# Norms without activation tables, normalisations fed between the gate's steps, and a stricter load order, in a one-layer decoder step

## The chip, the cores and the metric

One Trainium2 chip, all 8 cores, two dies (cores 0 to 3 and 4 to 7). Every core runs the same program on its own prompt of 2048 positions and 16 of the 128 sample rows; no data passes between cores. The time of a run is that of its slowest core, in microseconds of the device. Some runs fall into a second, slower state, in which the cores of a die have a lower granted clock: whole runs at 1229 to 1423 us. Engines are called PE (matrix), DVE (VectorE), ACT (ScalarE) and POOL (GpSimd). SBUF is a core's on-chip memory, PSUM the memory into which PE writes its sums.

## The reference, cut to what matters

```python
def rmsnorm(x, g):
    return x * rsqrt(mean(x * x, -1) + 1e-6) * g

xn = rmsnorm(h, g_mix); z = xn @ w_in                   # x_a B_a C_a | u v | g_a g_b
y_a = (b_a * dwconv3(c_a * x_a)) @ w_out_a
u, v = gelu(uv); v = rmsnorm(v, g_v)
y_b = (u * chunk_spatial(v)) @ w_out_b
h = h + (sigmoid(ga) * y_a + sigmoid(gb) * y_b) @ w_o
up = dwconv3(rmsnorm(h, g_ffn) @ w_up)
h = h + (gelu(fa) * fb) @ w_down
h = h + sigmoid(rmsnorm(h, g_ple) @ w_ple_gate) * (p @ w_ple)
y = rmsnorm(h, g_final)
```

So there are four norms over the 1024 channels on the residual stream: before the input projection (gain index 0), before the up-projection (1), before the gate (2) and at the end (3).

## The kernel before

A core makes two passes of 1024 positions (the first with the 16 sample rows), each cut into blocks of 384, 384 and 256 (or 272) columns. Channels lie on partitions, so `h` is 8 tiles of 128 channels. Weights stream as slabs through a ring of eight slots; a slab is loaded as soon as its slot is free and what `LOAD_AFTER` lists for it has landed. The program gives each engine its instructions as a queue; in the traces below an engine that waits for one holds all behind it.

A pass has these stages, by which the text below counts: the v projection with its spatial preparation (in pass 0 together with the start); then the convolution, the spatial gating, the merge and the output projection (called "conv to merge"); the up-projection; the down-projection; the gate. After the last gate stage only DVE and the stores are left: the tail.

The norm squares on ACT, adds the squares on POOL (or DVE), sums over partitions with matmuls with a matrix of ones, and takes the inverse root on ACT as exp(-0.5 ln x):

```python
def rstd(self, b):
    ...
    r, rr = rsR.get()
    P.op("act", ... r = Ln(pt + eps));  P.op("act", ... r = Exp(-0.5 * r))
    return r, rr

def to_xn(self, b, gi):                       # to_y does the same into h, and stores it
    r, rr = self.rstd(b)
    for k in range(8):
        P.op("dve", ... xn[k] = h[k] * g[gi, k] * r)
```

Ln and Exp are in another activation table than the tanh of the gate or the gelu of v, so each norm costs ACT a load of tables, and the next tanh or gelu another.

The start, and the loop of the gate:

```python
LOAD_AFTER[1] = [("h", 7, 0)]                 # slab 1 waits for all of the first block of x
load_h(0, block 0, 4); load_h(0, block 1, 4)
R.prefetch()                                  # slabs 0 .. 7
load_h(0, block 2, 2, <after slab 3>)
...
fn = Norm(p, "pool", delay=1)
for b in blocks:
    for i in range(8):
        # PE: gate projection and p @ w_ple; ACT: tanh; DVE: (tanh + 1) * pE
        P.op("dve", ... h[i] = 0.5 * tg + h[i])
        fn.add(i, b)                          # square and sum for the last norm
        if bi == 0 and i == 1: nrm.to_xn(b2, 2)
        if bi > 0 and i == 4:
            fn.to_y(blocks[bi - 1], 3, 2)
            if p == 0: load_h(1, blocks_of(1)[bi - 1], 2)
```

Of the kernel before, what the change touches and what calls it, by code (L numbers as in the profile page):

```python
# [162 lines left out]
def build_program():  # L163
# [9 lines left out]
    xt_d = [din("xt0", [128, 8, TT]), din("xt1", [128, 8, 1024])]  # L173
# [10 lines left out]
    yt_d = [dout("yt0", [128, 8, TT]), dout("yt1", [128, 8, 1024])]  # L184
# [5 lines left out]
    with es:  # L190
# [3 lines left out]
        h = sb("h", [128, 8, TT], F32)  # L194
# [14 lines left out]
        saT = sb("saT", [128, 8, 2, NS], F32)  # L209
        sfT = sb("sfT", [128, 44, 2, NS], F32)  # L210
        oAs = sb("oAs", [128, 8, NS], F32)
        oFs = sb("oFs", [128, 44, NS], F32)
# [22 lines left out]
        class PsRot:  # L235
            def __init__(self):
                self.i = 0

            def get(self):
                b = self.i % 8  # L240
                self.i += 1
                return ps[b], ("ps", b)
# [24 lines left out]
        def tiles_of(p):  # L267
            tl = [dict(t=t, rows=128, c0=t * 128, blk=t // 3) for t in range(8)]
            if p == 0:
                tl.append(dict(t=8, rows=NS, c0=1024, blk=2))  # L270
            return tl

# [90 lines left out]
        def proj(pt, ptr, wv, wres, u, p, b, halo=False):  # L363
            lo, hi = xcols(p, b, halo)
            bi = b["idx"]
            pairs = []
# [7 lines left out]
        class Norm:  # L374
            def __init__(self, p, eng, src=None, delay=0, early=False):
                self.early = early
                self.p, self.eng, self.delay, self.pe = p, eng, delay, False
                self.src = src or (lambda k, b: (h[:, k, b["c0"]:b["c0"] + b["n"] + b["s"]], [("h", k, b["idx"])]))
                self.cnt, self.slot, self.pend = {}, {}, []

            def add(self, k, b):
                self.pend.append((k, b))
# [3 lines left out]
            def _emit(self, k, b):  # L386
# [9 lines left out]
                if self.pe:  # L396
                    if q == 0:
                        self.bank = psR.get()
                    t, w = narR.get()
                    out = t.bitcast(BF16)[:, 0:N]  # L400
                    pt, ptr = self.bank
                    if q % 2:
                        P.op("dve", lambda e: e.tensor_tensor(out=out, in0=src, in1=src, op=ALU.mult), reads=rd, writes=w)
                    else:
                        P.op("act", lambda e: e.activation(out=out, in_=src, func=AF.Square), reads=rd, writes=w)
                    P.op("pe", lambda e: e.matmul(pt[:, 0:N], lhsT=ones[:], rhs=out, start=(q == 0), stop=(q == 7)),
                         reads=["ones"] + w, writes=[ptr])
# [9 lines left out]
                if 0 < q < 7:  # L417
# [9 lines left out]
            def rstd(self, b):  # L427
# [4 lines left out]
                pt, ptr = self.bank if self.pe else psR.get()  # L432
                if not self.pe:
                    group(pt[:, 0:N], [(ones[:], ssb[:, s, 0:N], [("ssb", s)]), (ones[:], sqb[:, s, 0:N], [("sqb", s)])], ["ones"], ptr)
                r, rr = rsR.get()
                P.op("act", lambda e: e.activation(out=r[:, 0:N], in_=pt[:, 0:N], func=AF.Ln, bias=epsT[:, 0:1]), reads=[ptr, "epsT"], writes=[rr])  # L436
# [3 lines left out]
            def to_xn(self, b, gi):  # L440
                bi, N = b["idx"], b["n"] + b["s"]
                r, rr = self.rstd(b)
                for k in range(8):
                    src, rd = self.src(k, b)
                    dst = xns[self.p][:, k, b["c0"] + 2:b["c0"] + 2 + N]
                    P.op("dve", lambda e, src=src, dst=dst, k=k: e.scalar_tensor_tensor(  # L446
                        out=dst, in0=src, scalar=gcol(gi, k), in1=r[:, 0:N], op0=ALU.mult, op1=ALU.mult),
                        reads=rd + [rr, "cst"], writes=[("xn", self.p, k, bi)])

            def to_y(self, b, gi, parts):  # L450
                bi, N, c0 = b["idx"], b["n"] + b["s"], b["c0"]
                r, rr = self.rstd(b)
                per = 8 // parts
                for q in range(parts):
                    for k in range(q * per, (q + 1) * per):
                        hv = h[:, k, c0:c0 + N]
                        P.op("dve", lambda e, hv=hv, k=k: e.scalar_tensor_tensor(  # L457
                            out=hv, in0=hv, scalar=gcol(gi, k), in1=r[:, 0:N], op0=ALU.mult, op1=ALU.mult),
                            reads=[("h", k, bi), rr, "cst"], writes=[("h", k, bi)])
                    store(yt_d[self.p][:, q * per:(q + 1) * per, c0:c0 + N], h[:, q * per:(q + 1) * per, c0:c0 + N],  # L460
                          f"y{bi}{q}", [("h", k, bi) for k in range(q * per, (q + 1) * per)])

        def load_h(p, b, parts, after=()):
            bi, N, c0 = b["idx"], b["n"] + b["s"], b["c0"]
            per = 8 // parts
            for q in range(parts):
                load(h[:, q * per:(q + 1) * per, c0:c0 + N], xt_d[p][:, q * per:(q + 1) * per, c0:c0 + N], f"h{bi}{q}",
                     [("h", k, bi) for k in range(q * per, (q + 1) * per)], reads=after)
# [9 lines left out]
        use_table(AF.Ln)  # L478
        LOAD_AFTER[1] = [("h", 7, 0)]
        load(cst[:], const_d[:, :], "cst", ["cst"])  # L480
        load_h(0, blocks_of(0)[0], 4)
        load_h(0, blocks_of(0)[1], 4)
        R.prefetch()
        load_h(0, blocks_of(0)[2], 2, R.item_slot[3][2])
# [13 lines left out]
        def setup_small():  # L498
# [3 lines left out]
            for j in range(8):  # L502
                P.op("pool", lambda e, j=j: e.tensor_scalar(out=Ds[:, j, :], in0=cst[0:NS, 204:220], scalar1=cst[0:NS, 196 + j:197 + j],
                                                            scalar2=None, op0=ALU.mult), reads=["cst"], writes=["Ds"])

# [132 lines left out]
        nextn = [None]  # L638
        for p in range(2):
# [3 lines left out]
            vit = None  # L643
# [7 lines left out]
            if p == 0:  # L651
                nrm = Norm(0, "dve")
# [8 lines left out]
                vit = [next_item() for _ in range(4)]  # L661
# [9 lines left out]
                v_of(2, 1)  # L671
                setup_small()
                setup_state()
                load(pT[:, :, :], pt_d[0][:, :, :], "pT", [("pT", b) for b in range(3)], eng="pool")
                P.op("pool", lambda e: e.tensor_copy(out=xns[1][:, :, 0:2], in_=xns[0][:, :, 1024:1026]),
                     reads=[("xn", 0, k, 2) for k in range(8)], writes=[("xnh", 1)])
            else:
                vit = [next_item() for _ in range(4)]
                for hf in range(2):
                    for bl in range(3):  # L680
                        v_of(bl, hf)
                        if hf == 0 and bl == 1:
# [338 lines left out]
```

## Time and profile before

| | before |
|---|---|
| time, median of 17 runs, slow ones included | 1226.59 us (1224.25 to 1310.7) |
| cores of the profiled run | 1215.5 to 1224.0 us |
| PE, DVE, ACT, POOL busy | 94, 57, 41, 30% |
| loads of activation tables on one core | 33 |

The profile's page gives busy shares and forty slices in time; the windows give busy time in chosen stretches; an engine's timeline lists its instructions in order, with the rest before each in brackets and what ended it; the waits sum those rests.

### The profile page before, as it was taken

The numbers are of one execution on the slowest core, as the hardware profiler recorded it, in microseconds if no ns is written. First come the engines' busy times: TensorE is split into PE (matmuls) and PEld (weight loads), VectorE is DVE, ScalarE is ACT, GpSimd is POOL, SyncE is SP. The second block draws the span as 40 slices with busy tenths as digits, with TensorE's granted clock in tenths as the row PEclk, the third lists the DMA queues.
The fourth block names the chain that finished last, engine by engine and source line by source line (L and its number), as shares of the span: only waits on it lengthen the run. The fifth ranks groups of instructions, "written<-read, shape, count | busy, mean of one in ns | idle before, by whom it ended". The sixth has DMA issues, their size and how long they took to land.

```text
span 1224.0 us, 24337 instructions; the slowest of 8 cores (1215.5 to 1224.0 us)
## 1 busy us (share of the span) xinstructions
PE 1146.2 (94%) x7852; PEld 761.5 (62%) x7852; DVE 701.0 (57%) x1354; ACT 497.3 (41%) x1031; POOL 362.8 (30%) x411
## 2 busy tenths in 40 slices
PE   4699999999999999999889999999998999999983
PEld 2566666666656666666467666666665666666642
DVE  3336674222589899534862567522248899951386
ACT  3552232121445565333566123211134555541264
POOL 3020101222534343355340010122243443334232
PEclk9899999999999999999889999999999999999997
DMA  9638562444464442665469736233335343135303
GB/s 190 156 51 107 84 104 41 69 70 70 70 98 71 77 70 48 138 117 108 69 165 195 160 70 120 54 70 70 70 70 87 70 87 71 25 74 97 70 16 138
DMA packets 46619, 109.68 MB, mean 90 GB/s; under 512 B 10240, under 2 KB 26112, under 8 KB 46496
## 3 DMA queue, kind: packets, MB, share of 16 engines
q0 software_dynamic: 22016, 82.86, 40.6%
q1 hardware_dynamic: 24480, 25.27, 7.7%
q8 instruction: 67, 1.10, 0.3%
q14 instruction: 56, 0.46, 0.1%
HBM read 181.01 MB, written 9.95 MB: 156 GB/s over the span
## 4 chain that ended last, share of the span: by engine, by line
PE 77%; DVE 8%; DMA 5%; ACT 4%; issue 4%; POOL 2%; DVEq 0%; SPq 0%; POOLq 0%; ACTq 0%
PE pq L356 66%; PE pq L837 10%; DVE s_xn L446 3%; DMA s_h<-xt 2%; DMA s_ring<-win 2%; DVE s_h L457 1%; POOL s_ss L419 1%; DVE s_wide L920 1%; ACT L436 1%; DVE s_h L922 1%; DMA s_wide<-gv 1%; ACT s_rsb L436 1%; PE pq L604 1%; ACT s_sq L416 1%; ACT s_rsb L437 0%
## 5 line engine op out<-in xcount | busy, mean ns | idle before, releaser
L356 PE MATMUL pq<-s_xn,s_ring 128*128 128x386 bf16 (+5 forms) x5184 | 791.4, 310 | 15.8 <-DVE s_wide L920 6.0
L356 PEld LDWEIGHTS pq<-s_xn,s_ring 128*128 128x128 bf16 x5184 | 500.8, 97 | 276.4 <-issue 25.4
L776 DVE SCALAR_TENSOR_TENSOR s_wide<-pq,s_cst,s_wide 128x384 f32<-128x384 f32 (+1 forms) x528 | 278.5, 568 | 30.6 <-ACT s_wide L768 2.2
L768 ACT ACTIVATE s_wide<-pq,s_cst 128x384 f32<-128x384 f32 (+1 forms) x264 | 137.3, 548 | 131.8 <-DVE s_wide L776 115.3
L783 POOL TENSOR_TENSOR s_R<-s_wide 128x1024 bf16<-128x1024 f32 x44 | 103.8, 2359 | 173.1 <-DVE s_wide L776 155.0
L837 PE MATMUL pq<-s_R,s_ring 128*128 128x384 bf16 (+2 forms) x1056 | 155.0, 309 | 0.0
L419 POOL TENSOR_TENSOR s_ss<-s_ss,s_sq 128x384 f32<-128x384 f32 (+2 forms) x105 | 99.0, 947 | 166.2 <-ACT s_sq L416 158.6
L633 DVE SCALAR_TENSOR_TENSOR s_wide<-s_wide,pq 128x384 f32<-128x384 f32 (+2 forms) x96 | 49.2, 513 | 172.8 <-PE pq L356 172.8
L837 PEld LDWEIGHTS pq<-s_R,s_ring 128*128 128x128 bf16 x1056 | 103.2, 98 | 50.8
L356 PE MATMUL pq<-s_R,s_ring 128*128 128x384 bf16 (+2 forms) x768 | 119.8, 309 | 0.0
L416 ACT ACTIVATE s_sq<-s_h 128x384 f32<-128x384 f32 (+2 forms) x120 | 57.5, 486 | 146.1 <-DVE s_h L843 70.3
L631 ACT ACTIVATE s_wide<-pq 128x384 f32<-128x384 f32 (+2 forms) x96 | 43.9, 458 | 176.8 <-PE pq L356 142.5
L356 PEld LDWEIGHTS pq<-s_R,s_ring 128*128 128x128 bf16 x768 | 75.0, 98 | 37.0
L635 POOL TENSOR_TENSOR s_xn<-s_wide 128x384 bf16<-128x384 f32 (+2 forms) x48 | 43.7, 911 | 166.6 <-DVE s_wide L633 166.6
L356 PE MATMUL pq<-s_ring,s_xn 128*128 128x256 bf16 (+1 forms) x544 | 74.7, 297 | 16.2 <-DVE s_xn L446 12.5
L446 DVE SCALAR_TENSOR_TENSOR s_xn<-s_h,s_cst,s_rsb 128x384 bf16<-128x384 f32 (+2 forms) x120 | 62.4, 592 | 40.7 <-ACT s_rsb L437 40.7
L843 DVE TENSOR_TENSOR s_h<-pq,s_h 128x384 f32<-128x384 f32 (+2 forms) x48 | 23.6, 513 | 99.1 <-PE pq L837 99.1
L356 PEld LDWEIGHTS pq<-s_ring,s_xn 128*128 128x128 bf16 (+1 forms) x544 | 56.4, 105 | 34.4 <-issue 24.1
L579 ACT ACTIVATE s_wide<-s_wide,s_cst 128x384 f32<-128x384 f32 (+1 forms) x48 | 27.8, 579 | 122.3 <-DVE s_wide L577 122.3
L581 DVE SCALAR_TENSOR_TENSOR s_wide<-s_wide,s_cst 128x384 f32<-128x384 f32 (+1 forms) x48 | 27.5, 573 | 38.0 <-ACT s_wide L579 36.8
L321 POOL DMA_DIRECT2D s_ring<-win x56 | 30.0, 543 | 63.2 <-PE pq L356 21.4
L782 ACT ACTIVATE s_wide<-s_wide 128x1024 f32<-128x1024 f32 x44 | 46.1, 1048 | 0.9 <-DVE s_wide L776 0.9
(97 smaller groups left out, 668.0 us busy)
## 6 DMA issues: line engine op xcount, KB each, us to landing
s_ring<-win POOLq DMA_DIRECT2D x56, 512.0 KB, 10.6
s_ring<-wup POOLq DMA_DIRECT2D x44, 512.0 KB, 9.0
s_ring<-wdn POOLq DMA_DIRECT2D x16, 704.0 KB, 8.3
yt<-s_h SPq DMA_DIRECT2D x8, 768.0 KB, 4.0
s_ring<-woa POOLq DMA_DIRECT2D x8, 512.0 KB, 11.3
s_ring<-wob POOLq DMA_DIRECT2D x8, 512.0 KB, 12.6
s_ring<-wo POOLq DMA_DIRECT2D x8, 512.0 KB, 11.0
s_ring<-wg POOLq DMA_DIRECT2D x8, 512.0 KB, 7.2
```

Source lines behind the costliest of these rows:

```text
L356: P.op("pe", lambda e, l=l, r=r, q=q: e.matmul(out, lhsT=l, rhs=r, start=(q == 0), stop=(q == n - 1)), reads=list(reads) + list(rd), write ...
L416: P.op("act", lambda e: e.activation(out=out, in_=src, func=AF.Square), reads=rd, writes=[w])
L419: P.op(self.eng, lambda e: e.tensor_tensor(out=dst, in0=acc, in1=out, op=ALU.add), reads=[sr, w], writes=[dw])
L446: P.op("dve", lambda e, src=src, dst=dst, k=k: e.scalar_tensor_tensor(out=dst, in0=src, scalar=gcol(gi, k), in1=r[:, 0:N], op0=ALU.mult, o ...
L631: P.op("act", lambda e, tt=tt, pg=pg: e.activation(out=tt[:, 0:N], in_=pg[:, 0:N], func=AF.Tanh, scale=0.5), reads=[pgr], writes=ttr)
L633: P.op("dve", lambda e, tt=tt, py=py: e.scalar_tensor_tensor(out=tt[:, 0:N], in0=tt[:, 0:N], scalar=1.0, in1=py[:, 0:N], op0=ALU.add, op1= ...
L635: P.op("pool", lambda e: e.tensor_tensor(out=xns[1 - p][:, i, c0 + 2:c0 + 2 + N], in0=ta[:, 0:N], in1=tb[:, 0:N], op=ALU.add), reads=tar + ...
L768: P.op("act", lambda e, acc=acc, pt=pt, cc=cc, c0=c0, n=n: e.activation(out=acc[:, c0:c0 + n], in_=pt[:, 2:2 + n], func=AF.Copy, scale=wcf ...
L776: P.op("dve", lambda e, acc=acc, pt=pt, cc=cc, c0=c0, n=n, tap=tap: e.scalar_tensor_tensor(out=acc[:, c0:c0 + n], in0=pt[:, tap:tap + n], ...
L782: P.op("act", lambda e: e.activation(out=aa[:, 0:1024], in_=aa[:, 0:1024], func=AF.Gelu_apprx_tanh), reads=aar, writes=aar)
L783: P.op("pool", lambda e: e.tensor_tensor(out=act[:, c, 0:1024], in0=aa[:, 0:1024], in1=bb[:, 0:1024], op=ALU.mult), reads=aar + bbr, write ...
L837: P.op("pe", lambda e, c=c: e.matmul(pD[:, 0:N], lhsT=wd[:, c, :], rhs=act[:, c, c0:c0 + N], start=(c == 0), stop=(c == 21)), reads=wdr + ...
```

## The change

Its intent is to take the table loads out of the norms, to let PE go on with the gate while DVE normalises, and to have less in the queues at the start and at the end. The core of the diff:

```diff
+    if gi in (0, 2, 3):        # inverse root on DVE: integer first guess, one Newton-like step
+        DVE  r  = int(-0.5 * int(pt) + 0x5F1FFFF9)
+        DVE  r2 = (-0.703952253 * r) * pt
+        DVE  r2 = r2 * r
+        DVE  r  = (r2 + 0.703952253 * 2.38924456) * r
+        return r, rr
...
-    for k in range(8): P.op("dve", ... xn[k] ...)
+    for k in range(8): bg.append(... job(k) ...)
+    if not spread: bg_flush(...)                    # otherwise: fed by bg_run between the gate's steps
...
-    LOAD_AFTER[1] = [("h", 7, 0)]
+    LOAD_AFTER[0] = [("h", 3, 0)]
+    LOAD_AFTER[1] = [("h", 3, 1)]
+    LOAD_AFTER[2] = [("h", 7, 2)]
-    load_h(0, blocks_of(0)[1], 4)
+    load_h(0, blocks_of(0)[1], 4, [("h", 7, 0)])
+    load_h(0, blocks_of(0)[2], 2, [("h", 7, 1)])
     R.prefetch()
-    load_h(0, blocks_of(0)[2], 2, R.item_slot[3][2])
...
-    fn = Norm(p, "pool", delay=1)
+    fn = Norm(p, "pool", delay=2)
+    fn.pe = p == 1                                  # pass 1: squares summed by matmuls with ones
...
-    h[i] = 0.5 * tg + h[i]                          # scalar_tensor_tensor
+    h[i] = tg + h[i]                                # tensor_tensor; p was halved once on POOL
     fn.add(i, b)
-    if bi == 0 and i == 1: nrm.to_xn(b2, 2)
-    if bi > 0 and i == 4: fn.to_y(blocks[bi - 1], 3, 2) ...
+    bg_run(-(-len(bg) // max(1, 7 - i)))
+    if bi == 0 and i == 0: nrm.to_xn(b1, 2, True)
+    if bi == 0 and i == 7: nrm.to_xn(b2, 2, True)
+    if bi > 0 and i == 1 and not (p == 0 and bi == 2): fn.to_y(blocks[bi - 1], 3, 2, True)
```

Besides: x and y are stored block by block, so that a load has one run per partition; the norms of the next pass's x move earlier in the down-projection; in pass 0 the outputs of the second block are written in the v stage of pass 1. `delay` is the number of gate steps by which the square of a result follows the result.

## The prediction

> **What bounds the kernel now.** I read the page first (busy shares and the 40 slices), then the windows by stage, then the tensor engine's timeline at each place where it rests, then the vector engine's timeline in the same places, and last the groups by form for durations. From the page:
>
> ```profile
> PE 1146.2 (94%) x7852; PEld 761.5 (62%) x7852; DVE 701.0 (57%) x1354; ACT 497.3 (41%) x1031; POOL 362.8 (30%) x411
> ...
> PE   4699999999999999999889999999998999999983
> ```
>
> The tensor engine (PE) is busy 94%. The mathematics in bulk is not touched, so only the missing 77.8 us, and the slow clock after each rest, can be won. The digits show where the rest is: the first two slices, a dip near slice 20, and the end. The windows by stage put numbers to it (columns: busy us of PE, weight loads, DVE, ACT, POOL; then clock, DMA share, GB/s):
>
> ```profile
> 0.00:74.34 74.34, 49.62 (x314) 33.32 (x315) 21.50 (x42) 37.83 (x66) 12.38 (x27) 0.91 0.67 143
> ...
> 325.00:346.00 21.00, 17.81 (x126) 11.94 (x124) 14.76 (x30) 8.07 (x19) 9.03 (x12) 1.00 0.04 8
> ...
> 579.30:630.57 51.27, 41.85 (x249) 25.55 (x246) 40.36 (x78) 31.09 (x60) 19.00 (x20) 0.87 0.49 101
> 630.57:664.10 33.53, 30.32 (x261) 25.91 (x259) 10.68 (x22) 22.77 (x40) 7.00 (x12) 0.95 0.89 185
> ...
> 1157.92:1205.27 47.35, 38.47 (x248) 23.88 (x245) 37.91 (x71) 28.73 (x55) 17.12 (x17) 0.96 0.16 46
> 1205.27:1224.00 18.73, 0.58 (x2) 0.21 (x2) 10.40 (x22) 7.34 (x14) 2.32 (x3) 0.62 0.39 140
> ```
>
> In order: the start (loads of x, first norm, the v projection of pass 0) has 24.7 us of PE rest; the gate stage of pass 0 (579 to 631) 9.4; the v projection of pass 1 3.2; the gate stage of pass 1 8.9; the tail 18.2. In the gate stages DVE is busy 40.4 of 51.3 and 37.9 of 47.4 us: it is close to being the bound itself. That decides most of this case. The row 325:346, the norm between merge and up-projection, rests 3.2 us, its twin at 910 rests 3.4, and the change leaves both alone.
>
> PE's timeline of the start (start us, us, operation, idle before and its releaser):
>
> ```profile
> 23.21 7.19 PE L356 MATMUL pq<-s_ring,s_xn 128*128 128x256 bf16 x40 [1.29 <-DMA s_ring<-win]
> ...
> 34.47 0.27 PE L356 MATMUL pq<-s_ring,s_xn 128*128 128x256 bf16 x1 [3.75 <-DVE s_xn L446]
> ...
> 59.57 14.84 PE L356 MATMUL pq<-s_ring,s_xn 128*128 128x256 bf16 x96 [4.02 <-DVE s_xn L446]
> ```
>
> The 4.02 us go back to the third block of x, whose load is held back until the fourth weight slab has landed (29 us), then shares the wires and lands at 44 to 47. In the gate stage of pass 0 and after it:
>
> ```profile
> 590.83 2.72 PE L356 MATMUL pq<-s_xn,s_ring 128*128 128x384 bf16 x8 [4.57 <-DVE s_wide L920]
> ...
> 649.32 14.93 PE L356 MATMUL pq<-s_ring,s_xn 128*128 128x256 bf16 x120 [2.17 <-DMA s_ring<-win]
> ```
>
> Here one sees a PE that waits for DVE, and then runs the same eight matmuls in 2.72 us that take 1.46 when warm. DVE, in turn, idles about 2 us before each norm:
>
> ```profile
> 594.47 4.13 DVE L446 SCALAR_TENSOR_TENSOR s_xn<-s_h,s_cst,s_rsb 128x272 bf16<-128x272 f32 x8 [2.00 <-ACT s_rsb L437]
> ...
> 614.59 5.06 DVE L457 SCALAR_TENSOR_TENSOR s_h<-s_h,s_cst,s_rsb 128x384 f32<-128x384 f32 x8 [2.07 <-ACT s_rsb L437]
> ```
>
> These idles are the wait for ScalarE's table load, Ln and Exp (1.28 + 0.58 + 0.52 us), and another 1.28 us load goes back to tanh.
>
> **What the Trainium skill says.** "ScalarE: Activation LUTs", section "What ACT_TABLE_LOAD costs", gives about 1283 ns per load, the same for every set; the trace has 1283 ns as the mean of every group of loads, and agrees. "TensorE: Matmul & The Clock Gate", Part 1, says that the array falls to half clock after an idle window of about 3.4 us and needs as much activity to come back; the 2.72 against 1.46 us after a 4.57 us rest agrees, so a removed rest is worth more than its own length. "GPSIMD Engine Reference", section 1 "Specifications", says that GpSimd shares its SBUF interface with VectorE instructions that have two SBUF inputs; eight normalisations of 128x384 take 5.06 us beside GpSimd's adds at 614 and 4.32 us at 582, which agrees. "VectorE: DVE Perf Modes", section on the perf-mode tier table, puts fp32 tensor_tensor at the plain rate; the trace has 0.56 us for it and for the scalar_tensor_tensor, so replacing the one by the other in the gate's residual add saves next to nothing.
>
> **The change part by part.**
>
> (a) Start. x is stored block by block, so a row of a load is 3072 contiguous bytes instead of two runs of 1536. The order becomes: first block of x, with slab 0 held until half of it is in; second block; slab 1 when half of that is in; third block; slab 2 when all x is in. Now slab 0 runs beside the first block (quarters at 5.3, 11.9, 12.7, 14.1 us). I reckon with 300 GB/s (the set-up moves about 14.6 MB by 50 us) and 2 us per dependent hop: first block at 9.5, second at 16.5, slab 1 at 21.5, third block at 25, slab 2 at 33, slab 3 at 38. PE needs slabs 0 and 1 for its first 48 matmuls: they start near 22 instead of 23.2, end at 29, then wait for the second norm as before, about 3 us; the next 96 (slabs 2 and 3 are in) end at 47, and the third norm is hidden behind 48 matmuls, so the 4.02 us rest and its cold clock (14.84 us for 96 matmuls against 10.77 for 96 at 630) vanish. End of the stage 64 to 66 instead of 74.3: minus 9 us.
>
> (b) Norm without tables. For all norms but the one before the up-projection, Ln and Exp become four DVE operations, each dependent on the one before. A dependent DVE pair in the trace starts 0.65 us apart at 384 columns, about 0.52 at 256: 2.6 and 2.1 us of DVE. The ACT wait of 1.8 to 2.2 us goes, but the DVE work is new: on DVE's own chain this is a loss of about 0.5 us per norm. The gain is that ACT no longer switches (tanh after the norm came 1.28 us late).
>
> (c) Spreading. The eight normalisations are fed between the gate's steps. In pass 0 those of the second output block are put off into the v projection of pass 1, where DVE is busy 10.7 of 33.5 us. Pass 0, by DVE: the early norm of the next x moves ahead of it; first block's normalisation done at 582; first block of the gate 1.1 + 2.6 + 13 = 16.7, second 2.1 + 8 pairs at 1.25 + 8 at 0.43 + 2.6 + 8 at 0.62 = 23, third 8 at 0.95 = 7.6: end at 631, PE about 629 instead of 630.6. Minus 2 us only. But GpSimd no longer waits behind the put-off work, so the slab that PE waited for at 649 is issued about 8 us earlier relative to PE's need: the 2.17 and 1.04 us rests and the slow clock go, 28.7 us for 256 matmuls against 33.5: minus 4 us.
>
> (d) The end. The last norm's sums go through 24 matmuls with ones (0.16 us each, in PE's spare time) instead of GpSimd adds. DVE from the last down-projection block, at 1153.3: four norms at 2.6 and two at 2.1 = 14.6; normalisations 8 at 0.53, 8 at 0.53, 8 at 0.40 = 11.6; outputs 4.4 + 4.4 + 3.2 = 12; pairs 16 at 1.13 and 8 at 0.87 = 25; tails and two short waits 2.2. Sum 65.4: DVE ends at 1218.7, where it now ends at 1221.55. Minus 2 to 3 us, with GpSimd quiet.
>
> Scaling p by a half on GpSimd, and the moved load of p, lie beside the spatial stage, off the path. Sum: 9 + 2 + 4 + 2.5 = 17.5; with a little for shorter queues elsewhere 19: 1226 - 19 = 1207.
>
> **The rivals.** First, DVE becomes the bound and nothing is won outside the start. For: my sums (c) and (d) leave DVE nearly without rest, and 72 operations are added. Against: its rests of 2 us are real and go. That makes 1215 to 1222. Second, the whole PE rest of the gate stages and the tail is won (9.4 + 8.9 + 18.2, plus clock), because spreading lets PE run ahead: for it, ACT loses eight tanh reloads; against it, DVE's sum. That makes 1185 to 1195. Third, the strict load order costs the start what it should win: each hop leaves the wires empty for about 2 us, and slab 1, which PE needs first, now waits for x. If it lands at 28, the start wins 3 us and the time is 1213. A small risk: more output and x traffic now lies in the v stage of pass 1, whose DMA share is already 0.89.
>
> **Range and chances.** The start is worth 3 to 12 us, the middle 2 to 10, the end -3 to 7. I predict 1207 us, and 1195 to 1218 should hold 8 times in 10. Over 2% faster means below 1201.5, which needs nearly all the upper ends: 0.27. Within 2%: 0.70. Slower by 2% would need a new stall that I don't see: 0.03.
>
> **What would show it.** PE's timeline: the v stage of pass 0 ending at 64 to 66 without a rest over 2 us before its last 96 matmuls; slab 1 landing near 22. The two gate stages: DVE busy over 90%, ACT without table loads, PE's stages still 45 us or more long. The v stage of pass 1 at about 29 us. The tail from PE's last gate matmul to the end is shorter than 18.7 us, but the gate stage of pass 1 longer. I am wrong if a gate stage of 40 us or less appears (DVE operations overlap better than dependent pairs show), or if the dependent four take over 3.5 us.

## The result, and the profile after

The changed kernel took 1208.24 us in the median of 10 runs (six fast ones from 1207.61 to 1208.31, four slow ones), the kernel before 1226.59 us. The ratio of the fast runs is 0.985, with an interval from 0.9839 to 0.9861. A ratio, here and below, is the mean time of one kernel's fast runs over that of the other's of the same rounds, so it is not quite the ratio of the medians quoted. Executions in which one die ran at a lower clock are left out of the means. The result is correct.

The page of the changed kernel, busy shares and PE's forty slices:

```profile
PE 1141.9 (95%) x7870; PEld 760.4 (63%) x7870; DVE 748.7 (62%) x1426; ACT 450.4 (37%) x969; POOL 353.1 (29%) x395
...
PE   3899999999999999999889999999999999999984
```

DVE has 48 us more work and ACT 47 us less. The dip of the first slices has not gone, the single 8 of slice 31 is now a 9, and the last slice is a 4 instead of a 3. The windows by stage of the changed kernel, in the same columns as those in the prediction (start; gate and v stage around the change of passes; last gate; tail):

```profile
0.00:70.55 70.55, 45.66 (x315) 32.52 (x315) 27.70 (x54) 28.70 (x55) 6.12 (x19) 0.95 0.75 159
...
571.31:622.81 51.50, 41.34 (x247) 24.32 (x247) 46.34 (x86) 18.73 (x43) 16.98 (x19) 0.93 0.37 84
622.81:651.31 28.50, 28.50 (x262) 25.45 (x260) 12.31 (x26) 18.84 (x36) 7.35 (x13) 1.00 0.90 185
1141.95:1194.55 52.60, 41.85 (x267) 24.70 (x264) 47.49 (x99) 19.92 (x47) 1.24 (x2) 1.00 0.17 56
1194.55:1206.10 11.55, 0.91 (x3) 0.29 (x3) 7.36 (x18) 1.50 (x4) 0.00 (x0) 0.61 0.41 159
```

Read DVE, the third of the busy columns: 46.3 of 51.5 us and 47.5 of 52.6 in the gate stages, which PE now spends with 10 us of rest each. The v stage of pass 1 has no rest at all. For the sum, I took the time of the first PE instruction of each stage on every core and the median over the eight, and took differences of these medians:

| stage | before | after | difference | predicted |
|---|---|---|---|---|
| start and v stage, pass 0 | 74.1 | 68.8 | -5.4 | -9 |
| conv to merge, pass 0 | 250.3 | 248.5 | -1.8 | 0 |
| up-projection, pass 0 | 173.4 | 173.5 | 0 | 0 |
| down-projection, pass 0 | 80.8 | 79.2 | -1.6 | 0 |
| gate, pass 0 | 49.6 | 51.3 | +1.7 | -2 |
| v stage, pass 1 | 33.2 | 28.5 | -4.7 | -4 |
| conv to merge, pass 1 | 245.0 | 243.1 | -1.9 | 0 |
| up- and down-projection, pass 1 | 247.9 | 247.7 | -0.3 | 0 |
| gate, pass 1 | 48.0 | 52.6 | +4.6 | together |
| tail | 17.8 | 11.4 | -6.4 | -2.5 |

Two cautions on this table. The up-projection is counted from the first sums of its norm, which stand some 14 us before its first matmul, inside the output projection. And where the cores are apart, a difference of medians books part of one stage to the next: the median of each core's own stage times gives +1.1 for the gate of pass 0 (not +1.7) and -3.7 for the v stage of pass 1 (not -4.7).

The differences sum to 15.8 us on the median core. The time is that of the slowest core and fell by 18.3; the other 2.5 us go with a smaller spread: the cores lay between 1215.5 and 1224.0 us before and lie between 1202.2 and 1206.1 now. The stages of each core show where the spread was. Before, PE waited 2.1 to 2.9 us for a weight slab in the v stage of pass 1 on cores 1, 2, 5 and 7, the four slowest (33.4 to 36.1 us in that stage), and at most 0.25 us on the others (30.6 to 31.1); conv to merge of pass 0 took 248.2 to 250.9. After, the v stage takes 28.5 us on every core and conv to merge of pass 0 248.2 to 248.7. What spread is left, 3.9 us, is that of the start, 66.6 to 70.5 us.

PE's timeline of the start, after; columns as in the prediction:

```profile
27.65 7.15 PE L376 MATMUL pq<-s_ring,s_xn 128*128 128x256 bf16 x40 [8.24 <-DMA s_ring<-win]
...
38.67 0.27 PE L376 MATMUL pq<-s_ring,s_xn 128*128 128x256 bf16 x1 [3.54 <-DVE s_xn L500]
...
54.42 5.84 PE L376 MATMUL pq<-s_ring,s_xn 128*128 128x256 bf16 x52
```

Slab 1 came at 27.6 us, and PE rested 8.24 us for it, where it had rested 1.29 before. (POOL, which issues the slabs, began its issue only at 20.53 us, after 11.13 us of waiting for x.) The rest for the second norm (3.5 us) is as it was. The third rest, of 4.02 us, is gone. Then the gate stage of pass 0:

```profile
591.72 0.32 PE L376 MATMUL pq<-s_xn,s_ring 128*128 128x384 bf16 x1 [1.95 <-DVE s_xn L500]
...
594.91 2.76 PE L376 MATMUL pq<-s_xn,s_ring 128*128 128x384 bf16 x8
```

PE still waits for DVE, now for normalised columns that are fed one by one, and eight matmuls still run at half clock (2.76 us). The norm itself, on DVE:

```profile
11.84 0.56 DVE L484 TENSOR_SCALAR s_rsb<-pq 128x384 int32<-128x384 int32 x1 [1.01 <-PE pq L438]
12.51 0.56 DVE L485 SCALAR_TENSOR_TENSOR s_sq<-s_rsb,pq 128x384 f32<-128x384 f32 x1
13.17 0.56 DVE L486 TENSOR_TENSOR s_sq<-s_sq,s_rsb 128x384 f32<-128x384 f32 x1
13.83 0.56 DVE L487 SCALAR_TENSOR_TENSOR s_rsb<-s_sq,s_rsb 128x384 f32<-128x384 f32 x1
14.57 4.32 DVE L500 SCALAR_TENSOR_TENSOR s_xn<-s_h,s_cst,s_rsb 128x384 bf16<-128x384 f32 x8 [0.18 <-DVE s_rsb L487]
```

From the first of the four to the normalisations are 14.57 - 11.84 = 2.73 us; 2.6 had been predicted.

### The profile page after: what moved, and what is told of

The parts are those of the page before. It is cut to its first block, busy times and chain, and to the rows that moved or that the text cites. A ratio compares the mean times of both kernels' runs of the same rounds, so it can differ in the third digit from the quotient of the medians.

```text
span 1206.1 us, 24352 instructions; the slowest of 8 cores (1202.2 to 1206.1 us)
## 1 busy us (share of the span) xinstructions
PE 1141.9 (95%) x7870; PEld 760.4 (63%) x7870; DVE 748.7 (62%) x1426; ACT 450.4 (37%) x969; POOL 353.1 (29%) x395
## 4 chain that ended last, share of the span: by engine, by line
PE 85%; DVE 8%; issue 3%; DMA 2%; ACT 1%; POOL 0%; DVEq 0%; SPq 0%; ACTq 0%; POOLq 0%
PE pq L376 73%; PE pq L913 11%; DVE s_xn L500 3%; DMA s_h<-xt 1%; DVE s_h L514 1%; DVE s_wide L1005 1%; PE pq L673 1%; DMA s_ring<-win 1%; DVE s_h L1008 0%; DVE s_sq L486 0%; DVE s_sq L485 0%; DVE s_rsb L484 0%; ACT s_sq L452 0%; DVE s_h L813 0%; DVE s_rsb L487 0%
## 5 line engine op out<-in xcount | busy, mean ns | idle before, releaser
L860 POOL TENSOR_TENSOR s_R<-s_wide 128x1024 bf16<-128x1024 f32 x44 | 103.8, 2358 | 173.5 <-DVE s_wide L853 164.1
L461 POOL TENSOR_TENSOR s_ss<-s_ss,s_sq 128x384 f32<-128x384 f32 (+2 forms) x90 | 83.7, 934 | 120.6 <-ACT s_sq L452 115.0
L452 ACT ACTIVATE s_sq<-s_h 128x384 f32<-128x384 f32 (+2 forms) x102 | 48.6, 487 | 146.6 <-DVE s_h L919 77.6
L376 PE MATMUL pq<-s_ring,s_xn 128*128 128x256 bf16 (+1 forms) x544 | 68.9, 287 | 18.0 <-DMA s_ring<-win 12.1
```

The lines of the kernel that those rows point to most:

```text
L376: P.op("pe", lambda e, l=l, r=r, q=q: e.matmul(out, lhsT=l, rhs=r, start=(q == 0), stop=(q == n - 1)), reads=list(reads) + list(rd), write ...
L452: P.op("act", lambda e: e.activation(out=out, in_=src, func=AF.Square), reads=rd, writes=[w])
L461: P.op(self.eng, lambda e: e.tensor_tensor(out=dst, in0=acc, in1=out, op=ALU.add), reads=[sr, w], writes=[dw])
L860: P.op("pool", lambda e: e.tensor_tensor(out=act[:, c, 0:1024], in0=aa[:, 0:1024], in1=bb[:, 0:1024], op=ALU.mult), reads=aar + bbr, write ...
```

## The experiments

Twelve kernels ran, each beside the kernel before on the same chip; all but one give the right result. The chip changes between groups of runs (x1 to x4, x5 to x8, x9 to x11, x12); the fast runs of the kernel before differ by under 0.6 us on average between these chips. A ratio is to the kernel before; the changed kernel has 0.985.

| run | edit | fast runs, us | ratio |
|---|---|---|---|
| x1 | slab 1 after the first block of x | 1208.15 to 1208.86 | 0.986 |
| x2 | also slab 2 after the second | 1202.35 to 1203.9 | 0.9817 |
| x3 | load order of before | 1203.92 to 1209.57 | 0.9841 |
| x4 | sums by matmuls in both passes | 1209.59 to 1210.01 | 0.987 |
| x5 | before, with the DVE norm alone | 1223.46 to 1226.58 | 0.9991 |
| x6 | before, without the gain loads of v | 1220.2 to 1220.81 | 0.9955 |
| x7 | x2 and x4, longer delays | 1202.31 to 1203.05 | 0.9808 |
| x8 | changed, with table norms | 1216.4 to 1218.57 | 0.9931 |
| x9 | x7, three of eight adds on POOL | 1197.19 to 1197.89 | 0.977 |
| x10 | changed, normalisations in one go | 1219.71 to 1220.89 | 0.9959 |
| x11 | changed, sums on POOL in both passes | 1212.58 to 1213.68 | 0.990 |
| x12 | x10 and x11 together | 1211.95, 1212.82 | 0.9891 |

### The start: x1, x2, x3 and x5

My theory for the start: the new load order is itself a loss, because slab 1 now waits for half of the second block of x. The rival: any order only moves the rest to another slab.

x1, slab 1 released by the first block:

```diff
-        LOAD_AFTER[1] = [("h", 3, 1)]
+        LOAD_AFTER[1] = [("h", 7, 0)]
```

> The changed kernel with one edit: weight slab 1 is released when the first block of x is in, not when half of the second is. In the changed kernel slab 1 lands at 27.6 us and PE rests 8.2 us for it. Theory A (the strict order costs the start: slab 1 waits for x that nobody needs yet): slab 1 lands at 20 to 22 us, PE's rest of 8.2 us falls below 3 us, the v stage of pass 0 ends 3 to 5 us earlier (68.8 us now, median core), total 1203 to 1205. Rival B (the wires are the limit, the same bytes must come first anyway): the rest only moves to the second norm or to slabs 2 and 3, the stage ends within 1.5 us of 68.8, total 1207 to 1209.

The time did not move: 1208.65 us. PE's timeline of x1 shows why:

```profile
23.13 6.21 PE L376 MATMUL pq<-s_ring,s_xn 128*128 128x256 bf16 x40 [3.38 <-DMA s_ring<-win]
...
45.22 1.03 PE L376 MATMUL pq<-s_ring,s_xn 128*128 128x256 bf16 x8 [2.05 <-DMA s_ring<-win]
48.46 6.74 PE L376 MATMUL pq<-s_ring,s_xn 128*128 128x256 bf16 x36 [2.20 <-DMA s_ring<-win]
```

The rest for slab 1 fell from 8.24 to 3.38 us, and two new rests came for slabs 2 and 3, which are still held until all of x has landed. Here the rival was right, but only because one gate was left in.

x2, slab 2 released by the second block as well:

```diff
-        LOAD_AFTER[1] = [("h", 3, 1)]
-        LOAD_AFTER[2] = [("h", 7, 2)]
+        LOAD_AFTER[1] = [("h", 7, 0)]
+        LOAD_AFTER[2] = [("h", 7, 1)]
```

> The changed kernel with slab 1 after the first block of x, and slabs 2 onwards after the second block instead of the third: the order in which PE needs them. Theory A: at least as good as slab 1 alone, v stage of pass 0 ends at 62 to 66 us, total 1202 to 1205. Rival B: slabs 2 to 7 now share the wires with the third block of x, which lands late as it did in the kernel before (44 to 47 us), so its norm is exposed again: the stage ends at 69 to 73, total 1208 to 1212.

It took 1203.26 us, and the start ends at 64.3 instead of 68.8. The same two places in x2:

```profile
23.63 6.12 PE L376 MATMUL pq<-s_ring,s_xn 128*128 128x256 bf16 x40 [3.32 <-DMA s_ring<-win]
...
48.84 6.39 PE L376 MATMUL pq<-s_ring,s_xn 128*128 128x256 bf16 x57
```

Each slab is now held only by what must land before it, and the later rests are gone.

x3, the order of before in the changed kernel (slab 0 free, the first two blocks of x at once, the third after slab 3):

```diff
-        LOAD_AFTER[0] = [("h", 3, 0)]
-        LOAD_AFTER[1] = [("h", 3, 1)]
-        LOAD_AFTER[2] = [("h", 7, 2)]
+        LOAD_AFTER[1] = [("h", 7, 0)]
-        load_h(0, blocks_of(0)[1], 4, [("h", 7, 0)])
-        load_h(0, blocks_of(0)[2], 2, [("h", 7, 1)])
+        load_h(0, blocks_of(0)[1], 4)
         R.prefetch()
+        load_h(0, blocks_of(0)[2], 2, R.item_slot[3][2])
```

> The changed kernel with the loading order of the kernel before (all else kept). Theory A (the order of loads is worth what the start won, 5.4 us by the median core's stage times): the v stage of pass 0 ends at 73 to 75 us again and the total is 1212 to 1215. Rival C (the start won by the DVE norm and the block layout with its longer rows, not by the order): the stage ends at 68 to 71 us and the total stays within 2 us of 1208.

The start ends at 64.9 us, 3.8 earlier than with the new order, although the third block of x is as late as it was before the change:

```profile
22.95 6.43 PE L376 MATMUL pq<-s_ring,s_xn 128*128 128x256 bf16 x41 [0.16 <-DVE s_xn L500]
...
48.52 6.72 PE L376 MATMUL pq<-s_ring,s_xn 128*128 128x256 bf16 x60
```

The total is less clear: its three fast runs spread over 5.7 us (1203.92, 1204.99, 1209.57), so its ratio only says that it is no slower than the changed kernel. The stage times of its trace carry the verdict: the new load order costs about 4 us, and the 4.02 us rest for the third norm goes away without it. So that rest had not been the late load. Neither expectation (73 to 75 us, or 68 to 71) had this.

x5 asks what it was, by putting the DVE norm alone into the kernel before, with nothing else:

```diff
+                if gi in (0, 2, 3):
+                    ... the four DVE operations ...
+                    return r, rr
-        use_table(AF.Ln)
+        use_table(AF.Gelu_apprx_tanh)
```

> The kernel before with part (b) alone: the norms' Ln and Exp become the four DVE operations; loads, layout, order of work all as before. The old loading order in the changed kernel ended the v stage of pass 0 at 64.9 us, against 74.1 in the kernel before and 68.8 in the changed one. Theory F (the start is won by taking the norm off ACT, whose queue of gelus, squares and table loads held the third norm's Ln until 57.7 us though its sum was ready at 50): the stage ends at 64 to 67 us here too, total 1213 to 1219. Rival G (the longer rows of the block layout bring the third block in earlier): the stage stays at 72 to 75. In the gate stages my prediction has a loss of about 0.5 us per norm on DVE against the tanh reloads saved: 48 to 52 us for pass 0.

The start ends at 66.5 instead of 74.1. The trace of the kernel before has the reason. PE's timeline gives the matmuls that sum the third block:

```profile
49.91 0.28 PE L356 MATMUL pq<-s_ssb,s_ones 128*128 128x272 bf16 x1
50.03 0.28 PE L356 MATMUL pq<-s_sqb,s_ones 128*128 128x272 bf16 x1
```

and ACT's timeline what it did then:

```profile
48.28 1.28 ACT L532 ACT_TABLE_LOAD   x1
...
56.20 0.19 ACT L539 ACTIVATION_READ_ACCUMULATOR s_wide<-s_R 128x1 f32 x1
56.40 1.28 ACT L436 ACT_TABLE_LOAD   x1
57.70 0.49 ACT L436 ACTIVATE s_rsb<-pq,s_epsT 128x272 f32<-128x272 f32 x1
```

The sum was ready by 50.3 us. Ln came at 57.7, because it stood in ACT's queue behind the gelus and squares of v, and behind a table load. The third block of x had landed long enough before. The norm on DVE does not stand in that queue.

As a whole, though, x5 gained nothing (ratio 0.9991, interval 0.997 to 1.0011), where theory F had 1213 to 1219 us. The 7.6 us of the start and 1.5 of the v stage of pass 1 were given back: gate of pass 0 +4.5 us, conv to merge of pass 1 +3.2, last gate +1.4. For the gates that agrees with DVE as their bound; the loss in the merge of pass 1 I did not trace further (by each core's own stage times it is only +1.1, the rest lies in the distance between the cores).

### The DVE norm undone: x8

```diff
-                if gi in (0, 2, 3):
+                if gi in ():
```

> The changed kernel with Ln and Exp on ACT again for all norms (part (b) undone, all else kept). Theory F: the v stage of pass 0 goes back to 72 to 76 us and the gate stages become shorter on DVE but wait 2 us per norm again; total 1211 to 1217. Rival: if the DVE operations only cost (DVE is the bound), the gate stages win 2.6 us per norm, and the total is 1204 or less.

The fast runs took 1216.4 to 1218.57 us, 9 to 10 us more than the changed kernel. (The profiled run fell into the slow state on cores 0 and 1; on the other six the start ends at 70.8 against 68.8, the gate of pass 0 takes 52.8 against 51.3 and that of pass 1 57.5 against 52.6 us.) The total is at the upper end of theory F, but its start is not: 2 us were lost there, not 3 to 7. So the norm is worth about 1 us put alone into the kernel before and about 10 us taken alone from the changed one. Half of the loss is in the last gate stage, where a table load and the reload for tanh stand before a tanh, and behind the tanh the square whose matmul PE waits for. A part of a change does not have a worth of its own.

### The stages that nobody had touched: x6

Both conv-to-merge stages had become 1.8 us shorter, which I had not predicted. Theory H: they had waited for the loads that spread the gain of v over all partitions (512 KB each), which had stood behind other things in the queue. The test takes these loads out of the kernel before; the products use another tile already there, so the outputs of v (two of the eight) are wrong, and the others right.

```diff
-                load(gvb[0:rows, 0:1024], gv_d.partition_broadcast(rows), "gvb", gvr)
-                ... in1=gvb ...
+                ... in1=bbc ...
```

> The kernel before without the two loads of the v gain by broadcast (the bias tile stands in for it, so the chunk-v outputs are wrong on purpose and all else is right). Theory H (the 1.8 us that the conv-to-merge stages of pass 0 and the 1.9 us that those of pass 1 became shorter, which I had not predicted, are DVE's waits for these loads, which landed after 11.8 and 9.8 us): those stages go from 250.3 and 245.0 us to 248 to 249 and 242.5 to 244 us, total 1221 to 1224. Rival I (they are PE's slow clock or cores' spread): no change over 0.5 us in either.

It took 1220.55 us; the two stages fell by 2.0 and 1.9 us, as much as the change had won there. (The total is 0.5 us under theory H's 1221 to 1224.) Theory H holds for what these loads cost. That in the changed kernel they do not cost it because they are issued earlier is read from the traces alone: in pass 1 the issue is 28.2 us into the stage before (at 692.25 us) and 21.4 us after (at 672.76), as its queue is no longer blocked as long by the outputs and loads that stand before it. DVE waited 10.0 us in all for the two loads before, and not at all after; from issue to landing they took 9.8 and 11.8 us before, 5.4 and 7.9 after.

### What bounds the gate stages: x4, x7, x9

Theory: DVE's amount of work bounds the gate stages, and POOL's adds lengthen the DVE instructions beside them. In the changed kernel the second block of the gate of pass 0 shows it. DVE's residual adds:

```profile
592.14 1.18 DVE L1008 TENSOR_TENSOR s_h<-s_wide,s_h 128x384 f32<-128x384 f32 x1
...
594.42 1.18 DVE L1008 TENSOR_TENSOR s_h<-s_wide,s_h 128x384 f32<-128x384 f32 x1
```

and POOL at the same time, adding squares:

```profile
591.92 0.99 POOL L461 TENSOR_TENSOR s_ss<-s_ss,s_sq 128x384 f32<-128x384 f32 x1 [1.28 <-ACT s_sq L452]
594.19 0.99 POOL L461 TENSOR_TENSOR s_ssb<-s_ss,s_sq 128x384 bf16<-128x384 f32 x1 [1.28 <-ACT s_sq L452]
```

These DVE adds, which start while POOL adds, take 1.18 us instead of 0.56 (others, less covered, 0.70 to 1.08). x4 sums the squares by matmuls in pass 0 too, so that POOL is quiet:

```diff
-            fn.pe = p == 1
+            fn.pe = True
```

> The changed kernel with the final norm's sums of squares on PE in both passes, so GpSimd is quiet in the gate stage of pass 0 too (24 matmuls of 0.16 us more there). Theory D (the gate stage of pass 0 won nothing because GpSimd's adds stretch DVE's residual adds: 1.08 to 1.18 us each from 588 to 595, 0.56 undisturbed): those adds fall to 0.56 us, the gate stage of pass 0 falls from 51.5 to 46 to 49 us, total 1204 to 1206. Rival E (DVE's bare operation count is the bound, or PE now waits for the squares on ACT as it does in pass 1): the stage stays at 50.5 to 52.5 us and the total within 1 us of 1208.

The adds fell to their plain duration:

```profile
590.73 0.56 DVE L1008 TENSOR_TENSOR s_h<-s_wide,s_h 128x384 f32<-128x384 f32 x1
...
592.39 0.56 DVE L1008 TENSOR_TENSOR s_h<-s_wide,s_h 128x384 f32<-128x384 f32 x1
```

and DVE was done with the second block 4.3 us earlier (613.9 against 618.2; in both, the first product of the stage is at 576.7). The time did not follow: 1209.86 us, and the gate stage of pass 0 took 53.6 us, more than the 51.3 of the changed kernel. Theory D (46 to 49) is refuted; the mechanism of rival E holds, with a longer stage than its 50.5 to 52.5. PE's waits say where it went, first those of the changed kernel:

```profile
PE pq L438 <- ACT s_wide L436: 16.6, 19, 4.3
PE pq L376 <- DVE s_xn L500: 13.2, 30, 3.5
```

and those of x4 (total us, times, longest):

```profile
PE pq L438 <- ACT s_wide L436: 23.3, 29, 4.5
```

Line 438 is the matmul that sums a square. In PE's queue it stands in order; if the square is not ready, everything behind it waits. In these sums over the whole run the waits for squares grew by 6.7 us: the gain of DVE became waits of PE. x7 gives these matmuls more time (the delay from two steps to four, and the output norm two steps later), with the load order of x2:

```diff
-            fn = Norm(p, "pool", delay=2)
-            fn.pe = p == 1
+            fn = Norm(p, "pool", delay=4)
+            fn.pe = True
-                    if bi > 0 and i == 1 and not (p == 0 and bi == 2):
+                    if bi > 0 and i == 3 and not (p == 0 and bi == 2):
```

> The changed kernel with the loads by need, the final sums on PE in both passes, and those sums delayed by four steps instead of two (and the output norm begun at step 3). With a delay of two PE cannot start a step until ACT has squared the result of two steps before: its rests for squares were 23 us in all in the run with PE sums in both passes, while DVE there had no stretched add left and finished the second block 4 us earlier. Theory J (the lost run-ahead ate that gain): with four steps PE's rests for squares fall below 8 us, the gate stage of pass 0 to 46 to 49 us, of pass 1 to 48 to 51, total 1194 to 1200. Rival K (DVE's count is the bound in both, run-ahead only moves the rest): the two gate stages together with the tail stay within 2 us, total 1202 to 1204.

The waits for squares fell to 12.2 us; the time is 1202.56, only 0.7 below x2: rival K, not theory J. The windows of x7 (both gate stages and the tail; core 2) show DVE as the busiest engine:

```profile
567.01:618.23 51.22, 44.02 (x269) 26.08 (x269) 45.54 (x95) 21.37 (x50) 4.53 (x9) 0.97 0.44 104
1137.27:1186.08 48.81, 40.61 (x266) 25.05 (x263) 44.05 (x91) 19.29 (x46) 1.23 (x2) 1.00 0.14 44
1186.08:1202.00 15.92, 1.39 (x6) 0.40 (x4) 11.03 (x26) 1.82 (x5) 0.00 (x0) 0.60 0.42 165
```

If DVE's amount of work is the bound, taking work off it must shorten the stages. x9 does that: POOL, now idle, makes three of the eight residual adds of each block.

```diff
-                    onpool = False
+                    onpool = i in (1, 3, 5)
```

> The kernel of x7 (loads by need, sums of squares through matmuls in both passes, a deeper delay), with three of the eight residual adds of each gate block on GpSimd instead of VectorE: 18 adds of 0.56 us (128x384) or 0.42 us (128x272) leave VectorE. Theory L (VectorE's count of work bounds the gate stages): VectorE loses about 1.6 us per block, so the gate stages get some 3 to 5 us shorter each (51.0 to about 47, gate of pass 1 plus tail from 64.2 to about 61), total 1195 to 1199. Theory M (the port that GpSimd shares with VectorE gives it back: a GpSimd add runs several times as long as VectorE's and stretches the VectorE instructions beside it from 0.56 to 1.1 us): VectorE's busy time in the gate stages stays within 1.5 us, and the sums of squares, which need the added block, come later: total 1202 to 1207.

It took 1197.3 us (fast runs 1197.19, 1197.34, 1197.89), 5 us less than x7, and its ratio of 0.977 is the only one here over 2% from the kernel before. Its windows for the same stages, core 2 again:

```profile
566.93:615.97 49.04, 42.48 (x269) 25.50 (x269) 43.37 (x86) 21.46 (x50) 13.91 (x17) 1.00 0.48 107
1134.66:1181.09 46.43, 40.62 (x266) 25.03 (x263) 42.16 (x83) 19.33 (x46) 9.95 (x10) 1.00 0.15 46
1181.09:1196.40 15.31, 1.39 (x5) 0.40 (x4) 11.09 (x25) 1.81 (x5) 0.97 (x1) 0.65 0.44 171
```

DVE's busy time fell by 2.2 and 1.9 us, and the stages by 2.2 and 2.4: theory L in kind, though less than its 3 to 5 us a stage. The nine adds that moved are about 4.7 us of DVE by their plain durations (six of 0.56, three of 0.44), so more than half of that was paid back, as theory M has it, in DVE instructions beside POOL's: in the gate stage of pass 0 those with both inputs in SBUF got longer (at 384 columns, normalising the outputs went from 610 to 705 ns, normalising for the gate from 612 to 660, the adds that stayed from 558 to 607), while the product that reads PSUM stayed at 547. The groups of x9 by form show that a POOL add costs 2.2 times what it does on DVE at rest, not "several times" as I had written:

```profile
L1008 POOL TENSOR_TENSOR s_h<-s_wide,s_h 128x384 f32<-128x384 f32 x12 | 14.5, 1211 | 42.3 <-DVE s_wide L1005 42.3
...
L1008 DVE TENSOR_TENSOR s_h<-s_wide,s_h 128x384 f32<-128x384 f32 x20 | 12.1, 606 | 2.4 <-DVE s_wide L1005 0.5
```

### Spreading, and the sums by matmuls: x10, x11, x12

x10 takes the spreading away: each norm's eight operations are issued in one go.

```diff
-    fn.to_y(blocks[bi - 1], 3, 2, True);  nrm.to_xn(b1, 2, True);  nrm.to_xn(b2, 2, True)
+    fn.to_y(blocks[bi - 1], 3, 2);        nrm.to_xn(b1, 2);        nrm.to_xn(b2, 2)
```

> The changed kernel with the eight normalisations of a norm issued in one go, as before, instead of fed between the steps of the gate. Theory N (spreading as such matters little, because VectorE has the same work either way and PE waits for its sum): total 1207 to 1210, the gate stages within 1 us of 51.3 and 52.6. Theory O (spreading is what lets PE run beside the norm): each norm in a gate stage is a burst of about 2.6 + 4.5 us in which no bank of the gate is freed, PE rests 2 us or more in front of the next gate matmuls with a cold clock after it, 3 to 4 times in the two stages: gate of pass 0 at 54 to 57, total 1213 to 1219.

1220.5 us, 12 more than the changed kernel, though not where theory O had put it: the gate of pass 0 kept its 51.2 us, and all of the loss is in the gate of pass 1, 66.8 us against 52.6. Only pass 1 sums by matmuls. DVE's timeline in x10:

```profile
1177.12 4.32 DVE L514 SCALAR_TENSOR_TENSOR s_h<-s_h,s_cst,s_rsb 128x384 f32<-128x384 f32 x8
...
1182.02 0.56 DVE L1008 TENSOR_TENSOR s_h<-s_wide,s_h 128x384 f32<-128x384 f32 x1
```

and PE's:

```profile
1156.59 0.48 PE L438 MATMUL pq<-s_wide,s_ones 128*128 128x384 bf16 x1 [5.73 <-ACT s_wide L436]
...
1174.18 0.48 PE L438 MATMUL pq<-s_wide,s_ones 128*128 128x384 bf16 x1 [3.30 <-ACT s_wide L436]
...
1183.39 0.48 PE L438 MATMUL pq<-s_wide,s_ones 128*128 128x384 bf16 x1 [2.65 <-ACT s_wide L436]
```

A burst of a norm holds DVE for some 7 us with the four operations before it, from 1174.4 to 1181.4. The residual add comes after it, then the square on ACT, then its matmul, and PE, which is only two steps ahead, stands still. Each of these rests is followed by matmuls at half clock; the window of the stage has a clock of 0.85 instead of 1.00.

x11 leaves the spreading and puts the sums of pass 1 back on POOL:

```diff
-            fn.pe = p == 1
+            fn.pe = False
```

> The changed kernel with the last norm's sums of squares on GpSimd in pass 1 too, as in pass 0 (no matmuls with ones in the second gate stage). Theory P (as predicted: GpSimd quiet makes VectorE's chain shorter at the end): VectorE's adds in the second gate stage go up to 1.1 us, gate of pass 1 plus tail from 64.0 to 66 to 68, total 1210 to 1213. Theory Q (the squares' matmuls cost PE as much, as the 23 us of rests for them in x4 suggest): gate of pass 1 shorter by 1 to 3 us on PE, tail longer by as much, total 1207 to 1209.

1213.3 us: theory P, as predicted in part (d), with a little more than its numbers. Gate of pass 1 and tail take 55.7 + 14.1 = 69.8 us against 64.0.

x12 has both edits, to see whether the losses add.

```diff
-            fn.pe = p == 1
+            fn.pe = False
-    fn.to_y(blocks[bi - 1], 3, 2, True);  nrm.to_xn(b1, 2, True);  nrm.to_xn(b2, 2, True)
+    fn.to_y(blocks[bi - 1], 3, 2);        nrm.to_xn(b1, 2);        nrm.to_xn(b2, 2)
```

> The changed kernel with both undone: normalisations issued in one go (as in x10) and the last sums of squares on GpSimd in both passes (as in x11). By themselves the two cost about 12.5 us (x10) and 5 us (x11). Theory R (spreading is needed only because the matmuls of the squares stand in PE's queue in order: when a burst of a norm on VectorE delays the square, everything behind its matmul waits; without those matmuls PE runs ahead of the burst): gate of pass 1 plus tail 66 to 68 as in x11 (69.7), not 76.6 as in x10; total 1211 to 1216. Theory S (the burst itself starves PE of free banks, so the two costs add): gate of pass 1 plus tail near 80, total 1222 to 1228.

They do not: the two fast runs took 1211.95 and 1212.82 us (the other four, and with them the profiled one, were slow on one die). On the six undisturbed cores of the profiled run, gate of pass 1 and tail take 55.2 + 13.2 = 68.4 us. Theory R holds:

| gate of pass 1 and tail, us (ratio of the kernel) | fed between the steps | in one go |
|---|---|---|
| squares summed by matmuls | 64.0 (0.985) | 77.0 (0.9959) |
| squares summed on POOL | 69.8 (0.990) | 68.4 (0.9891) |

Spreading by itself is worth nothing here or costs a little. Sums by matmuls by themselves cost nearly 9 us. Together they win 4. The one is needed because the other puts PE's queue behind DVE's.

## Why the prediction was right or wrong

The time was right within 1.2 us (1207 against 1208.24), and so was "within 2%". That it came so close is luck: some 8 us of terms that were too large (start 3.6, gate of pass 0 3.7, end 0.7) cancelled some 7 us of terms that were too small or missing (untouched stages 3.8, spread of the cores 2.5, v stage of pass 1 0.7).

**(a) The start, -9 predicted, -5.4 measured: mis-sized, with a wrong cause in it.** The step that failed is "slab 1 at 21.5": it landed at 27.6, PE rested 8.24 us for it, and the third rival, "If it lands at 28, the start wins 3 us", described the load order rightly. The size that was wrong is the rate: "300 GB/s (the set-up moves about 14.6 MB by 50 us)" is misread, for the trace of the kernel before has 10.2 MB by 50 us, 203 GB/s. So x came late: the issue of slab 1, which waits for half of the second block, began at 20.53 us, where the sum had the whole block in at 16.5. Then the wires stood nearly empty (DMA share 0.02 from 20.5 to 23 us; the "2 us per dependent hop" had been put in without a number from a trace, and was about right), and the slab landed 7.1 us after its issue. x3 shows that the order by itself costs about 4 us, and x2 that letting each slab go by need wins them back. The step "The 4.02 us go back to the third block of x" failed too: x5 removes the rest with the loads as they were; it was Ln in ACT's queue, 7.4 us behind its input. With the old order the changed kernel's start ends 9.2 us earlier than before (x3), about the 9 that I had predicted, most of it by the norm (7.6 us in x5) and none by the order of loads; the new order gives 3.8 of them back.

**(b) The norm on DVE.** The 2.6 us were right (2.73 measured from the first of the four to the normalisations). What was not right was its place in the account, "on DVE's own chain this is a loss of about 0.5 us per norm", with a gain only for tanh. In the kernel before its largest gain was at the start. Its worth depends on the rest of the change: 1 us alone (x5), 10 us when removed from the whole (x8).

**(c) Gate of pass 0, -2 predicted, +1.7 measured: wrong.** That DVE bounds it was right: 46.3 of 51.5 us busy. The term that was too small is "first block of the gate 1.1 + 2.6 + 13 = 16.7, second 2.1 + ... = 23", together 39.7 us of DVE: from the end of the first normalisation (574.9) to the end of the second block (618.2) the trace has 43.3. The third block took 8.4 us against 7.6. That is 4.4 us too little in the sum, against an error of 3.7 in the stage. (The written sum also has a slip: 582 + 16.7 + 23 + 7.6 is 629.3, not 631.) In the sum a pair in the second block had 1.25 us; in the trace, its add alone takes 1.08 to 1.18 us beside POOL's. x4, where POOL is quiet, ends the two blocks 4.3 us earlier. **The v stage of pass 1**, -4 predicted, -4.7 measured: right, and with the reason that was given, no rest and full clock in 28.5 us; POOL issues the next five slabs 3.2 us into the stage, where it had done so after 8.4 (5 us earlier, not the predicted 8).

**(d) Gate of pass 1 and tail, -2.5 predicted, -1.8 measured: right.** The tail became shorter and the stage longer, as written. x11 bears out "with GpSimd quiet": sums on POOL would cost 5.8 us here. That this rests on the spreading (x10) was not foreseen.

**The missing terms.** "A little for shorter queues elsewhere" was 1.5 us; it turned out as 5.3: 1.8 and 1.9 in the conv-to-merge stages, which x6 traces to the loads of v's gain, and 1.6 in the down-projection of pass 0. In the latter, two PE rests of 0.38 and 0.90 us that were ended by POOL are gone, as the sums for the next x are emitted earlier; that is read from the traces and not tested. And 2.5 us are the smaller spread of the cores, which the stage times of each core put down to the v stage of pass 1 and conv to merge; the sum was made for one core and had no term for it.

**The rivals.** The first, DVE as the bound outside the start, is what x7 and x9 show for the gate stages (in x4 and x10 PE's waits for the squares bound them instead); but its total (1215 to 1222) was too high, as the v stage and the untouched stages won 10 us. The second fell: 10 us of PE rest remain in each gate stage. In a kernel that loads by need, keeps POOL's adds away from the sums and gives some of DVE's work to POOL, 1197 us come out (x9), 2 us above that rival's range; so part of the rest was to be had, but not by feeding alone.

## What to carry to other kernels

When a norm's wait goes, look at which queue it stood in: here an Ln waited 7.4 us behind unrelated work of its engine, while the late load that seemed to be the cause was harmless. Count the work of the engine next in line before taking a wait away; what shortened the gate stages in the end was fewer operations on DVE, not another order of them. And if an intermediate result goes through an in-order queue, as the squares through PE, then its producer must never be held up for longer than the queue's lead; two edits that only work together should be tested as a square of four kernels, not one by one.

## What the Trainium skill lacked or had wrong

- "GPSIMD Engine Reference", section 1 "Specifications", names the contention with VectorE instructions of two SBUF inputs; that section gives no size. Here a 128x384 fp32 add on DVE takes 0.56 us alone and 1.08 to 1.18 us beside an add of the same size on GpSimd (0.99 us); with GpSimd making three of eight adds, over half of the 4.7 us taken from DVE was lost again.
- "ScalarE: Activation LUTs", section "What ACT_TABLE_LOAD costs", adds a drain of about 1380 ns to the 1283 ns of a load, some 2.66 us per switch. No such gap shows here: an ACT instruction of 0.19 us started at 56.20, the load at 56.40, and Ln at 57.70, so the switch cost 1.3 us of the engine's time.
- "TensorE: Matmul & The Clock Gate", Part 1, advises to budget 13/16 of the clock (1.95 GHz) for dense matmuls on all cores. The fast runs here, with all eight cores at work and PE busy 95% of the time on the profiled one, hold a granted clock of 0.98 to 0.99. A die near 0.81 does occur, in slow runs (two of x12, with such a die at 0.81 to 0.82, took 1414 and 1416 us), but 46 of the 65 recorded runs of the changed kernel and the experiments were fast, and the slow ones mostly had a higher clock than that.
- I found no page with the time between two VectorE instructions of which one needs the other's result: at 128x384 fp32 they start 0.66 us apart, and eight independent ones 0.54 us apart (4.32 us in all, the last of 0.56), so the inverse root in four dependent steps pays about 0.12 us at each.
